# Delta rule in a four-layer decoder trunk: keys first, and one inversion of all sixteen systems on VectorE

## The chip, the core and the metric

The kernel runs on one core of one Trainium2 chip. A core has a matrix engine (TensorE; in the profile PE, with its weight loads as PEld), a vector engine (VectorE, DVE), an activation engine (ScalarE, ACT), a general engine (GpSimd, POOL) and a queue engine (SyncE, SP) that issues the transfers of this kernel. The metric is the device time of one execution in microseconds; lower is better. Before the change three runs took 1253.02, 1254.41 and 1255.75 us.

## The reference, cut to what matters

Four layers, each `x += mixer(rmsnorm(x))`, then `x += conv_ffn(rmsnorm(x))`, for 256 tokens of width 1024. Layer 2 has the mixer that changes, a gated delta rule with 8 heads of width 128:

```python
proj = h @ w_in                                   # queries, keys, values, gates
qkv = silu(causal_dwconv(proj[..., :3 * d], conv_w))
a_mat = where(strict, (k_beta @ k.T) * decay, 0)  # per head and chunk
t_mat = triangular_solve(a_mat + eye, eye)        # its inverse
u = t_mat @ v_beta
w = t_mat @ (k_beta * exp(gc))
v_new = u_i - w_i @ state                         # chunk by chunk
o_i = q_i @ state + a_i @ v_new
state = state * sd_i + k_i.T @ v_new
out = (rmsnorm(o) * silu(z)) @ w_o
```

The kernel takes chunks of 128 tokens, so there are 8 heads times 2 chunks = 16 unit triangular systems of 128 unknowns, each of which has to be inverted before the values can be corrected.

## The kernel before, in words

**Products.** All weights stream from DRAM in chunks of 8 tiles of 128x128 (`Stream`, L102). SP loads a chunk into `wraw` (L128, 4 buffers); ScalarE rounds it into `whi` (L150) and VectorE takes the exact rest `wlo` (L151), at most 5 chunks ahead of their use (L161). A tile costs TensorE three matmuls of 256 columns (L360 to L362); all of TensorE's instructions are recorded on the helper lines L252 and L255.

**Order.** TensorE's instruction order is written out by hand by `Weave` (L169): products are the fill, and every other step is a generator that yields what it cost TensorE and what it waits for, a time by the plan's own clock or a name. When the plan's clock reaches that point, the step's next instructions are put into TensorE's order, whether or not the data will be there by then. The other engines' orders, and SP's, come from a scheduler that goes by the order of the program and by what is ready.

**The delta rule** (`gdn`, L551). Sixteen jobs of 16 tiles each (L17: q0 to q7, then v and z mixed) make, with `queries_keys` (L650), queries and keys of one head per job, with `values` (L825) and `gate` (L943) two heads per job. On VectorE a job takes one multiply out of PSUM (L653, L832) and six steps of two convolutions (L392). `gates` (L578) and `decays` (L632) make write strengths and decay matrices. The heads are worked on in two halves of four (`half`, L892):

- `lengths` (L662): four transposes a head, then squares with sums on ScalarE (L680).
- `systems` (L696): one product a chunk gives the system and the scores together (L705, scaled on VectorE at L709). The systems go to DRAM (L717).
- `invert` (L726): the blocks of 16 on the diagonals come back one block to a partition, 64 partitions (L732). GpSimd inverts them by substitution (L740 to L745). The result goes to DRAM (L747) and returns as rows (L750).
- `join16` (L762): inverses of blocks of 32 from those of 16: two products for every system (L769, L780), with masks on VectorE (L723, L772, L789) and transposes (L760).
- `join_half` (L798): blocks of 64, then of 128.
- then the corrections of both chunks (L903 to L935), the norm (`finish`, L868) and the output's parts (`output`, L950).

The last product (`residual`, L368) takes its first half of rows once heads 0 to 3 are done ("o0") and its second half once heads 4 to 7 are ("o1").

Of the kernel before, what the change touches and what calls it, by code (L numbers as in the profile page):

```python
# [9 lines left out]
F32 = mybir.dt.float32  # L10
# [18 lines left out]
BLK = 16  # L29
NB = 6  # L30
# the jobs of the delta rule's products, in their order
GDN_FILL = "q0 q1 q2 q3 q4 q5 q6 q7 v0 z0 v1 v2 v3 z1 z2 z3"
PRIO = (1, 0)
# [6 lines left out]
L_QK, L_V, L_LEN, L_SYS, L_BLOCKS, L_JOIN, L_XI, L_PM, L_OUT = 6.0, 6.0, 1.0, 0.5, 6.0, 13.0, 1.0, 2.5, 1.0  # L40

# columns of the packed per-channel parameters
# [9 lines left out]
# columns of the shape-only constants  # L52
# [5 lines left out]
C_BD = C_NEG + P  # L58
C_LV = C_BD + P
C_UP = C_LV + P  # L60
C_EO = C_UP + P
C_ST = C_EO + 2
# [3 lines left out]
def constants():  # L66
# [11 lines left out]
    b = i // BLK  # L78
    c[:, C_BD:C_BD + P] = b[:, None] // 2 == b[None, :] // 2
    lower = (b[:, None] == b[None, :] + 1) & (b[:, None] % 2 == 1)  # L80
    c[:, C_LV:C_LV + P] = np.where(lower, -1.0, 0.0)
    c[:, C_UP:C_UP + P] = lower.T
    c[:, C_EO:C_EO + 2] = b[:, None] % 2 == np.arange(2)[None, :]
# [14 lines left out]
# the heads whose queries and keys are made at the same time: the first products follow x as it comes  # L98
# [3 lines left out]
class Stream:  # L102
    """The weights, 8 tiles of 128x128 to a chunk, in the order of their use.

    A chunk is loaded ahead of its use and split into two parts that one pass of the tensor
    engine carries each: hi is w rounded to 12 bits, lo the exact rest."""
# [49 lines left out]
    def take(self, n=1):  # L156
        """The next n tiles side by side: (hi, lo), each [128, n * 128]."""
# [59 lines left out]
def trunk(ctx: ExitStack, tc: tile.TileContext, xT, wstream, pvec, cst, wba, hv, out):  # L217
# [15 lines left out]
    half8 = keep.tile([P, 2, 8], F32, name="half8")  # L233
# [3 lines left out]
    warm = keep.tile([P, 8], F32, name="warm")  # L237
# [9 lines left out]
    class Tensor:  # L247
        """The tensor engine; remembers its last instruction."""
# [9 lines left out]
    # the tensor engine's clock rises while the first data comes  # L258
# [6 lines left out]
    def after(inst):  # L265
        """No earlier in the order of its engine than the tensor engine's last instruction."""
# [30 lines left out]
    def squares(n, apart=KB):  # L297
        """The squares of block n, added to the others' unless n is one of the last, kept apart."""
# [43 lines left out]
    def product(ps, n, rh, rl):  # L342
        """ps[128, 256] += the next n tiles, against rh[k] + rl[k]."""
# [24 lines left out]
    def residual(n_k, rh, rl, gain, order, needs=None):  # L368
        """x += the product, in the order of the plan."""
# [18 lines left out]
    def conv(y, u, taps):  # L388
        """y = causal depthwise convolution of u along its free axis; taps: columns, last first."""
# [156 lines left out]
    # With b the write strength, D the decays between the tokens of a chunk and k the keys before  # L546
    # they are scaled to unit length, the chunk's corrections w solve a unit lower triangular system
    # (I + s_j k_i.k_j D_ij) w = r; s_j = b_j / |k_j|^2 makes up for the lengths. All four heads' systems
    # of a half are worked on together; the blocks of 16 on their diagonals are inverted by
    # substitution, one block to a partition, and joined into larger ones by products.  # L550
    def gdn(gain):  # L551
        nm = Norm()
        NS = 2 * G_H
        with tc.tile_pool(name="gdn", bufs=1) as pool, \
# [17 lines left out]
            def big(dt=F32):  # L572
                return pool.tile([P, NS, P], dt, name="big", bufs=NB)
# [4 lines left out]
            def gates():  # L578
# [44 lines left out]
                for s in halves:  # L623
                    yield from decays(s)
# [463 lines left out]
```

## Time and profile before

| | |
|---|---|
| Median of 3 runs | 1254.41 us |
| The profiled execution, first to last instruction (its span; no other time of it is given) | 1253.2 us |
| TensorE matmuls, busy | 1236.0 us |
| VectorE, busy | 945.0 us |
| ScalarE, busy | 730.2 us |
| GpSimd, busy | 103.4 us |
| TensorE's clock, mean | 0.991 |
| The delta rule on TensorE: first product to last | 581.7 to 760.4 us |

Matmuls are pipelined: in the timeline a matmul of 256 columns lasts 0.28 us, but the next one begins 0.12 us later. Costs on TensorE are therefore taken from the distance of starts and not from durations. The same holds, to a smaller degree, for VectorE. "Idle before" is time in which an engine had nothing to do just before an instruction; the name behind the arrow is what it waited for last.

### The profile page before, as it was taken

What the parts mean: (1) busy time and instruction counts of PE and PEld (TensorE: products, weight loads), DVE (VectorE), ACT (ScalarE), POOL (GpSimd) and SP (SyncE); (2) the same over time, 40 slices, a digit from 0 to 9 for tenths busy, and PEclk for the clock granted to TensorE, in tenths of its full rate; (3) what the DMA queues carried; (4) which work ended last, traced back from release to release, by engine and by line L of the source; (5) the groups of instructions that cost most, each with busy time, mean ns of one, the idle gap of its engine ahead of it and who ended that gap; (6) DMA issues with size and microseconds to landing.
All of it is one profiled execution on the core that took longest, in us unless ns stands there. A gap on an engine that the chain in (4) does not pass through costs nothing.

```text
span 1253.2 us, 25399 instructions
## 1 busy us (share of the span) xinstructions
PE 1236.0 (99%) x10222; PEld 1218.7 (97%) x10222; DVE 945.0 (75%) x1532; ACT 730.2 (58%) x1259; POOL 103.4 (8%) x147
## 2 busy tenths in 40 slices
PE   9999999999999999999998999999999999999997
PEld 8989999999999999999997999999999989999997
DVE  7756999856877999855995568999665756999842
ACT  6655766544445666545873666666554655766641
POOL 2002000001002000002055002000011002000000
PEclk9999999999999999999997999999999999999998
DMA  8655565656656556665444345666655445565650
GB/s 293 195 155 165 185 185 185 185 185 185 185 185 182 177 188 183 195 183 176 130 126 127 87 135 157 201 184 186 187 187 181 153 160 167 178 185 186 184 185 35
DMA packets 67430, 216.01 MB, mean 172 GB/s; under 512 B 11248, under 2 KB 14832, under 8 KB 67312
## 3 DMA queue, kind: packets, MB, share of 16 engines
q1 hardware_dynamic: 67024, 213.86, 55.1%
q8 instruction: 80, 1.31, 0.4%
q10 hardware_dynamic: 288, 0.52, 0.1%
q14 instruction: 38, 0.31, 0.1%
HBM read 212.13 MB, written 2.23 MB: 171 GB/s over the span
## 4 chain that ended last, share of the span: by engine, by line
PE 90%; DVE 4%; ACT 2%; issue 2%; POOL 1%; DMA 1%; SPq 0%; POOLq 0%; DVEq 0%; ACTq 0%
PE mm L252 84%; PE sm L252 5%; DVE wlo L151 1%; PE sm L255 1%; DVE xl L290 1%; DVE yqk L392 1%; POOL xm L743 1%; ACT whi L150 1%; POOL xb L745 1%; ACT jk L680 0%; DMA wraw<-wstream 0%; DVE x L380 0%; DVE big L643 0%; DMA xc<-d 0%; ACT yqk L658 0%
## 5 line engine op out<-in xcount | busy, mean ns | idle before, releaser
L151 DVE TENSOR_TENSOR wlo<-wraw,whi 128x1024 fp32r<-128x1024 f32 (+1 forms) x404 | 490.5, 1214 | 198.3 <-ACT whi L150 197.1
L252 PE MATMUL mm<-xh,whi 128*128 128x256 f32 x2112 | 603.4, 286 | 0.0
L252 PE MATMUL mm<-xl,whi 128*128 128x256 f32 x2112 | 595.9, 282 | 0.7 <-DVE xl L290 0.7
L252 PE MATMUL mm<-xh,wlo 128*128 128x256 f32 x2112 | 595.7, 282 | 0.6 <-DVE wlo L151 0.6
L150 ACT CAST whi<-wraw 128x1024 fp32r<-128x1024 f32 (+1 forms) x404 | 420.2, 1040 | 294.3 <-PE mm L252 264.2
L252 PEld LDWEIGHTS mm<-xl,whi 128*128 128x128 f32 x2112 | 400.1, 189 | 1.8 <-DVE xl L290 1.1
L252 PEld LDWEIGHTS mm<-xh,wlo 128*128 128x128 f32 x2112 | 399.8, 189 | 1.3 <-DVE wlo L151 1.0
L252 PEld LDWEIGHTS mm<-xh,whi 128*128 128x128 f32 x2112 | 400.0, 189 | 1.1 <-ACT whi L150 0.3
L252 PE MATMUL mm<-ah,whi 128*128 128x256 f32 x704 | 198.1, 281 | 0.0
L252 PE MATMUL mm<-ah,wlo 128*128 128x256 f32 x704 | 198.1, 281 | 0.0
L252 PE MATMUL mm<-al,whi 128*128 128x256 f32 x704 | 198.1, 281 | 0.0
L392 DVE SCALAR_TENSOR_TENSOR y<-u,pv,y 128x255 f32<-128x255 f32 (+1 forms) x352 | 146.0, 478 | 0.0
L252 PEld LDWEIGHTS mm<-ah,whi 128*128 128x128 f32 x704 | 132.5, 188 | 0.0
L252 PEld LDWEIGHTS mm<-al,whi 128*128 128x128 f32 x704 | 132.5, 188 | 0.0
L252 PEld LDWEIGHTS mm<-ah,wlo 128*128 128x128 f32 x704 | 132.5, 188 | 0.0
L304 POOL TENSOR_TENSOR sq<-sq 128x256 f32<-128x256 f32 x62 | 51.2, 825 | 980.0 <-ACT sq L302 978.1
L385 ACT CAST ah<-a 128x256 fp32r<-128x256 f32 x88 | 35.7, 406 | 99.8 <-DVE a L412 99.8
L390 ACT ACTIVATE y<-u,pv 128x256 f32<-128x256 f32 x176 | 79.6, 500 | 8.6 <-DVE u L405 8.6
L405 DVE TENSOR_TENSOR u<-mm,rb 128x512 f32<-128x512 f32 x88 | 60.5, 688 | 2.7 <-PE mm L252 1.3
L290 DVE SCALAR_TENSOR_TENSOR xl<-x,pv,xh 128x256 fp32r<-128x256 f32 x64 | 53.2, 862 | 3.1 <-ACT xh L289 3.1
L410 ACT ACTIVATE y<-y 128x256 f32<-128x256 f32 x88 | 36.6, 418 | 19.6 <-DVE y L392 17.4
L380 DVE TENSOR_TENSOR x<-x,mm 128x512 f32<-128x512 f32 (+1 forms) x36 | 22.4, 623 | 24.6 <-PE mm L252 24.6
(197 smaller groups left out, 1145.0 us busy)
## 6 DMA issues: line engine op xcount, KB each, us to landing
wraw<-wstream SPq DMA_DIRECT2D x396, 512.0 KB, 3.6
wraw<-wstream SPq DMA_DIRECT2D x8, 256.0 KB, 4.5
x<-xT SPq DMA_DIRECT2D x8, 128.0 KB, 4.3
d<-aq SPq DMA_DIRECT2D x2, 512.0 KB, 3.6
out<-xg ACTq DMA_DIRECT2D x2, 256.0 KB, 2.3
cs<-cst SPq DMA_DIRECT2D x1, 329.0 KB, 6.4
pv<-pvec SPq DMA_DIRECT2D x1, 324.5 KB, 5.5
cs<-cst SPq DMA_DIRECT2D x1, 320.0 KB, 5.6
```

The source lines that it names most:

```text
L150: self.nc.scalar.copy(hi[:, s], raw[:, s])
L151: self.nc.vector.tensor_sub(lo[:, s], raw[:, s], hi[:, s].bitcast(F32))
L252: self.last = nc.tensor.matmul(*a, **k)
L255: self.last = nc.tensor.transpose(*a, **k)
L290: V.scalar_tensor_tensor(xl[n], xn, col(gain + n), xh[n].bitcast(F32), op0=ALU.mult, op1=ALU.subtract)
L304: G.tensor_add(sums[0], sums[0], sq)
L380: V.tensor_add(xn, xn, pss.pop(n)[:, :w * T].rearrange("p (g t) -> p g t", g=w))
L385: S.copy(dst_h, src)
L390: S.activation(y, u, AF.Copy, scale=col(taps[0]))
L392: V.scalar_tensor_tensor(y[:, d:], u[:, :T - d], col(c), y[:, d:], op0=ALU.mult, op1=ALU.add)
L405: V.tensor_mul(u, pairs(ps), nm.rb2)
L410: S.activation(y[:, 0, :], y[:, 0, :], AF.Silu)
```

## The change

The jobs become k0 to k3, v0 to v3, q0 to q3, z0 to z3, with two heads in each. The keys of all heads come first, and only keys are needed for the systems. `keys` multiplies keys by keys and takes the squared lengths from that product's diagonal, on VectorE; it scales the system on VectorE and stores the four diagonal blocks of 32 with one transfer each. `queries` makes the scores apart from the systems. `invert` works on all 16 systems at once, 64 blocks of 32, each on two partitions that hold its even and its odd rows, so that all 128 partitions are used; the substitution is 31 steps of two instructions, now on VectorE. `join16` with its masks, `am`, `pm` and its products is gone. `join_half` takes 16 systems instead of 8. The result of the joins leaves PSUM through VectorE for `xt` and through ScalarE for `xi`. Some instructions are marked to go ahead of their place in the program (`tc.high_priority()`).

```diff
-BLK = 16
-GDN_FILL = "q0 q1 q2 q3 q4 q5 q6 q7 v0 z0 v1 v2 v3 z1 z2 z3"
+BLK = 32
+GDN_FILL = "k0 k1 k2 k3 v0 v1 v2 v3 q0 q1 q2 q3 z0 z1 z2 z3"
+L_GATES, L_KEYS, L_QK, L_V, L_BLOCKS, L_JOIN, L_XI, L_OUT = 8.0, 3.0, 6.0, 6.0, 6.0, 8.0, 2.0, 1.0
...
+            def keys(n, ps):
+                yield 0, ("norm",)
+                y = kk[:, n:n + 2, :]
+                mixed(1, n, ps, y)
+                yield 0, ("decays",)
                 S.activation(y, y, AF.Silu)
+                yield 0, L_KEYS
...
+                for i in range(4):
+                    h, ts = n + i // 2, slice(i % 2 * P, (i % 2 + 1) * P)
+                    PE.matmul(pk[:, i * P:(i + 1) * P], lhsT=kk[:, h, ts], rhs=kk[:, h, ts], start=True, stop=True)
...
+                with tc.high_priority():
...
+                        V.tensor_tensor_reduce(out=jk, in0=pk[:, i * P:(i + 1) * P], in1=ident, scale=1.0, scalar=0.0,
+                                               op0=ALU.mult, op1=ALU.add, accum_out=ln[:, 1, m:m + 1])
+                    V.tensor_scalar(le[:, 1, ms], ln[:, 1, ms], EPS, None, op0=ALU.add)
+                    V.reciprocal(sk[:, ms], le[:, 1, ms])
...
+                        V.scalar_tensor_tensor(aq[:, m, :], pk[:, i * P:(i + 1) * P], sk[:, m:m + 1],
+                                               dt[:, m, :], op0=ALU.mult, op1=ALU.mult)
+                    for b in range(NQ):
+                        bs = slice(b * BLK, (b + 1) * BLK)
...
+                            nc.sync.dma_start(out=o["d1"][b, ms].rearrange("m j c -> j m c"), in_=aq[bs, ms, bs])
+                wv.set(f"k{n}", LAG)
+                yield 0.9, L_KEYS
...
+            def invert():
...
+                yield 0, tuple(f"k{n}" for n in range(0, H, 2))
+                G.tensor_tensor(rn[:, 1, :], le[:, 1, :], half8[:, 1, :], op=ALU.pow)
+                wv.set("lengths", 2 * LAG)
+                for s in range(2):
+                    nc.sync.dma_start(out=bl[s * 64:(s + 1) * 64], in_=o["d1"].rearrange("b m j c -> (b m) j c"))
+                yield 0, L_BLOCKS
+                busy = 0.0
+                for k in range(BLK - 1):
+                    n, r = k // 2 + 1, BLK - 1 - k
+                    m = xm[:, :n * r].rearrange("p (n r) -> p n r", n=n)
+                    first = V.tensor_mul(m, xb[:, :n, k:k + 1].to_broadcast([P, n, r]),
+                                         bl[:, k:k + 1, k + 1:].to_broadcast([P, n, r]))
+                    if busy == 0:
+                        after(first)
+                    V.tensor_sub(xb[:, :n, k + 1:], xb[:, :n, k + 1:], m)
+                    busy += 2 * (0.16 + n * r / 960)
+                    if busy > 2.5 or k == BLK - 2:
+                        yield 0, 1.5 * busy
+                        busy = 0.0
+                d2 = dram.tile([2, NQ, NS, BLK // 2, BLK], F32, name="d2")
+                nc.sync.dma_start(out=d2.rearrange("s b m i c -> (s b m) i c"), in_=xb)
...
+                    for b in range(NQ):
+                        for s in range(2):
+                            nc.sync.dma_start(out=x32[b * BLK + s:(b + 1) * BLK:2],
+                                              in_=d2[s, b].rearrange("m i c -> i m c"))
+                yield 0, L_JOIN
...
+                    after(V.transpose(xi32.rearrange("p m i -> p (m i)"), x32.rearrange("p m i -> p (m i)")))
...
+                yield 0, L_XI
+                yield from join_half(BLK, (0, 64), (0,), lambda r, m: xi32[r, m, :], lambda r, m: x32[r, m, :], xi, xt)
+                yield from join_half(64, (0,), (), lambda r, m: xi[:, m, :], lambda r, m: xt[r, m, r], xi, xt)
+                wv.set("inverse", LAG)
```

## Rows read from the trace of the kernel before

**Rows 1.** The page, busy time (share of the span) and instructions of each engine.

```profile
PE 1236.0 (99%) x10222; PEld 1218.7 (97%) x10222; DVE 945.0 (75%) x1532; ACT 730.2 (58%) x1259; POOL 103.4 (8%) x147
```

**Rows 2.** The chain of waits, 636 to 668 us: start, length, what.

```profile
637.85 2.92 DMA d<-aq
640.79 2.75 DMA bl<-d
...
660.34 1.96 DMA d<-xb
662.31 3.19 DMA xc<-d
```

**Rows 3.** Timeline of PE: start, length, form, count, [idle before, releaser].

```profile
581.73 0.28 PE L252 MATMUL mm<-xh,whi 128*128 128x256 f32 x1
...
627.60 0.65 PE L255 MATMUL sm<-cs,yqk 128*128 128x128 f32 x4 [1.03 <-ACT yqk L658]
...
633.97 0.65 PE L255 MATMUL sm<-cs,yqk 128*128 128x128 f32 x4 [0.28 <-ACT jk L680]
...
666.58 3.56 PE L252 MATMUL sm<-xi,big 128*128 128x16 f32 x16 [4.32 <-DVE xi L760]
...
679.06 1.07 PE L252 MATMUL sm<-xi,aq 32*32 32x32 f32 x32 [0.46 <-DVE xi L760]
...
684.31 0.69 PE L252 MATMUL sm<-xt,m 32*32 32x32 f32 x16 [0.84 <-ACT big L817]
...
760.33 0.28 PE L252 MATMUL mm<-big,wlo 128*128 128x256 f32 x1
```

**Rows 4.** Stretches: busy time of each engine, TensorE's clock, DMA share, GB/s.

```profile
592.80:637.80 45.00, 43.68 (x356) 42.56 (x355) 41.03 (x95) 39.65 (x99) 3.43 (x2) 1.00 0.43 132
...
655.00:660.00 5.00, 5.00 (x37) 4.79 (x37) 4.93 (x12) 2.72 (x6) 4.29 (x10) 1.00 0.00 0
...
665.00:670.00 5.00, 3.42 (x17) 3.45 (x17) 2.86 (x5) 0.98 (x1) 1.11 (x1) 0.50 0.99 369
670.00:675.00 5.00, 5.00 (x24) 5.00 (x25) 3.05 (x3) 1.01 (x2) 0.49 (x3) 0.50 0.57 112
```

**Rows 5.** Timeline of PE, a product of `join16` and what follows it.

```profile
698.61 1.85 PE L252 MATMUL sm<-xi,big 128*128 128x16 f32 x16
700.31 1.14 PE L252 MATMUL sm<-m,kt 128*128 128x128 f32 x8
```

**Rows 6.** The chain of waits, a stretch of layer 1 with products alone.

```profile
404.23 184.05 PE mm L252 x1554
```

**Rows 7.** Timeline of DVE, the four kinds of its larger work.

```profile
592.84 0.69 DVE L653 TENSOR_TENSOR u<-mm,rb 128x512 f32<-128x512 f32 x1 [2.79 <-ACT rb L337]
...
611.93 3.44 DVE L643 SCALAR_TENSOR_TENSOR big<-sm,gc,cs 128x128 f32<-128x128 f32 x13
...
618.16 2.45 DVE L392 SCALAR_TENSOR_TENSOR yqk<-u,pv,yqk 128x255 f32<-128x255 f32 x6
...
641.84 2.36 DVE L151 TENSOR_TENSOR wlo<-wraw,whi 128x1024 fp32r<-128x1024 f32 x2
```

**Rows 8.** Groups by line and form, DVE: busy us, mean ns of one.

```profile
L455 DVE CUSTOM_DVE_ANT_0 p<-sm,nb 128x128 f32<-128x128 f32 x16 | 4.6, 290 | 9.8 <-PE sm L252 8.0 <-PE sm L255 1.7
...
L455 DVE DVE_READ_ACCUMULATOR2_ANT st<- 128x1 f32 x32 | 2.7, 83 | 0.0
...
L782 DVE TENSOR_TENSOR xt<-xt,sm 128x128 f32<-128x128 f32 x2 | 0.6, 288 | 2.5 <-PE sm L252 2.5
...
L691 DVE TENSOR_TENSOR sk<-sk,bt 128x8 f32<-128x8 f32 x2 | 0.3, 168 | 0.1
```

**Rows 9.** Timeline of SP, the store and the load after the inversion.

```profile
660.34 0.49 SPq L747 DMA_DIRECT2D d<-xb  x1
...
662.31 0.38 SPq L750 DMA_DIRECT2D xc<-d  x1
```

**Rows 10.** Timeline of ACT, the weight rounding at 665 us.

```profile
664.94 1.04 ACT L150 CAST whi<-wraw 128x1024 fp32r<-128x1024 f32 x1 [5.49 <-DMA wraw<-wstream]
```

More of the change, by code (lines that the diff above doesn't have):

```diff
@@ L648, in decays @@
-                wv.set(f"d{s.h0}")
-            def queries_keys(h, ps):
-                yield 0, ("norm",)
+                    with tc.high_priority():
+                        for i in range(4):
+                            h, t = divmod(m0 + i, 2)
+                            V.scalar_tensor_tensor(dt[:, m0 + i, :], pd[:, i * P:(i + 1) * P],
+                                                   gc[:, t, h:h + 1], cs[:, C_NEG:C_NEG + P],
+                                                   op0=ALU.subtract, op1=ALU.add)
@@ new lines, in gates, with mixed @@
+                    yield 0.9, 0
+                with tc.high_priority():
+                    V.tensor_sub(dl, gc[:, 2, :], gc[:, 0, :])
+                    for m in (0, H):
+                        S.activation(dt[:, m:m + H], dt[:, m:m + H], AF.Exp)
+                    S.activation(dl, dl, AF.Exp)
+                    S.activation(eg, gc[:, 1, :], AF.Exp)
+                    V.tensor_scalar(neg, eg, -1.0, None, op0=ALU.mult)
+                wv.set("decays")
+            def mixed(q, n, ps, y):
@@ L833, in values @@
+            def values(n, ps):
+                yield 0, ("norm",)
                 y = pool.tile([P, 2, T], F32, name="u", bufs=4)
-                for q in range(2):
-                    conv(y[:, q, :], u[:, q, :], taps(2, h + q))
+                mixed(2, n, ps, y)
                 S.activation(y, y, AF.Silu)
                 yield 0, L_V
-                yield 0, (f"l{s.h0}",)
+                yield 0, ("lengths",)
+                if n == 0:
+                    o["r"] = big().rearrange("p (t a) i -> p t a i", t=2)
@@ new lines, in m4, with heads @@
+            def m4():
+                return pool.tile([P, G_H, P], F32, name="m4", bufs=NM)
+            def heads(s, one):
+                ps = bank("sm")
+                for a in range(G_H):
+                    one(ps[:, a * P:(a + 1) * P], G_H * s + a)
+                return ps
+            def solve(s, t):
+                pw = heads(s, lambda p, h: PE.matmul(p, lhsT=o["xt"][:, 2 * h + t, :], rhs=o["r"][:, t, h, :],
+                                                     start=True, stop=True))
+                w = m4()
@@ L887, in finish @@
[L887 to L901 removed]
+                V.tensor_mul(f[:, 1, :], f[:, 1, :], rq)
@@ L903, in half @@
                 w = solve(s, 0)
                 yield 0.87, LAG
-                pst = bank("sm")
-                for a in range(G_H):
-                    PE.matmul(pst[:, a * P:(a + 1) * P], lhsT=s.kt[:, a, :], rhs=w[:, a, :], start=True, stop=True)
-                st = pool.tile([P, G_H, P], F32, name="m4", bufs=6)
-                S.copy(st.rearrange("p a i -> p (a i)"), pst)
-                po = scores(s, 0, w)
-                yield 1.74, LAG / 2
-                wv.add(finish(s, 0, po.rearrange("p (a i) -> p a i", a=G_H)))
@@ L923, in half @@
[L923 to L928 removed]
+                pst = heads(s, lambda p, h: PE.matmul(p, lhsT=kt[:, h, :], rhs=w[:, h % G_H, :], start=True, stop=True))
@@ new lines, in chunks @@
+                st = m4()
+                S.copy(st.rearrange("p a i -> p (a i)"), pst)
+                yield 0.87, (f"q{G_H * s}", f"q{G_H * s + 2}")
+                wv.add(finish(s, 0, four(scores(s, 0, w))))
+                yield 0.87, LAG / 2
+                ps = heads(s, lambda p, h: PE.matmul(p, lhsT=kk[:, h, P:], rhs=st[:, h % G_H, :], start=True, stop=True))
+                for a in range(G_H):
+                    h = G_H * s + a
+                    V.scalar_tensor_tensor(o["r"][:, 1, h, :], ps[:, a * P:(a + 1) * P], neg[:, h:h + 1],
+                                           o["r"][:, 1, h, :], op0=ALU.mult, op1=ALU.add)
@@ L929, in half @@
+                pq = heads(s, lambda p, h: PE.matmul(p, lhsT=qq[:, h, P:], rhs=st[:, h % G_H, :], start=True, stop=True))
+                qs = m4()
+                V.tensor_mul(qs, four(pq), eg[:, hs].unsqueeze(2).to_broadcast([P, G_H, P]))
                 yield 1.74, LAG
@@ L971, in fill @@
                     yield from products([ps], range(KB), KB, xh, xl)
-                    if job == "q0":
+                    n = 2 * int(job[1:])
+                    if job == "k0":
                         wv.add(nm.steps())
                         wv.add(gates())
-                        for n in PRIO:
-                            wv.add(half(halves[n]))
-                    n = int(job[1:])
-                    wv.add({"q": queries_keys, "v": values, "z": gate}[job[0]](n if job[0] == "q" else 2 * n, ps))
+                        wv.add(invert())
+                        for s in range(2):
+                            wv.add(chunks(s))
+                    wv.add({"k": keys, "q": queries, "v": values, "z": gate}[job[0]](n, ps))
                 yield from residual(KB, yhs, yls, gain, PLAN_HALVES, {0: ("o0",), KB // 2: ("o1",)})
```

482 lines of the change are left out of this document (184 added, 298 removed).

## The prediction, on record before the changed kernel was run

> **What bounds the kernel now.** I read the page first. TensorE's matmuls are busy 99% of the span, its weight loads 97%, VectorE 75% [rows 1]. Read alone, this says that work taken from TensorE is won and work given to VectorE is free. But the share is a mean over all layers, so the next view is the delta rule's own stretches. It runs on TensorE from 581.7 to 760.4 us, 178.7 us in all [rows 3]. In the 45 us from its first norm on, VectorE is busy 41.03 and ScalarE 39.65 [rows 4]: two engines nearly full beside TensorE. Third, the chain of waits. From the last system at 637.85 it runs through two transfers of 2.92 and 2.75 us, GpSimd's substitution until 660.34, and two more transfers of 1.96 and 3.19 [rows 2]. It is that chain for which TensorE waits 4.32 us at 666.58; with four smaller waits it stands still 1.03 + 0.28 + 4.32 + 0.46 + 0.84 = 6.9 us [rows 3]. Behind the long wait its granted clock is 0.50, the 1.2 GHz level, from 665 to 675, in which it works 3.42 + 5.00 = 8.4 us [rows 4]; at the 2.4 GHz level that work takes half, so 4.2 us are lost.
>
> **What TensorE gains.** `join16` goes. One of its four products over 8 systems takes 700.31 - 698.61 = 1.70 us at full clock [rows 5], so 6.8 us. Key and query products cost the same in two pieces of 128 columns as in one of 256 (I take it so from the columns). 24 transposes of keys and queries stand where 32 stood: four take at most 0.65 [rows 3], so 8 give up to 1.3, and I take 0.7, as they overlap. If no wait at all were left, the delta rule would take 178.7 - 6.9 - 4.2 - 6.8 - 0.7 = 160.1 us. The most to be won is thus 18.6 us.
>
> **Where TensorE stands in its new order.** Its order is fixed by the plan's clock. Adding up the plan's yields by hand gives the places: all four key products behind tile 70 of the 256 tiles of fill, the values' transposes behind tiles 102, 116, 132 and 148, the scores of the first two query jobs behind 164 and 178, and the first product of the joins behind tile 188. A tile is three matmuls of 184.05 / 1554 = 0.118 us [rows 6], 0.355 us. Up to the joins TensorE has 188 tiles, 66.8 us; 40 products for decays, keys and scores, four in at most 1.14 us [rows 5] and in 0.95 as they overlap, 9.5; 32 transposes at 0.1, 3.0; norm, gates and changes of kind, by estimate 5.2 (what before needs beyond tiles and products). The sum is 84.5, so without a wait it is there at 666.2 us, and has 160.1 - 84.5 = 75.6 us behind it.
>
> **What VectorE must have done by then.** Since TensorE's order holds the values' transposes and two score products ahead of the joins, VectorE has to finish all of this first, in whatever order. It begins at 592.84 with the first multiply [rows 7].
> - Weight parts: 24 chunks used, 8 of them made before: 16 at 1.14 us (two in 2.36, the overlap counted once) [rows 7]: 18.2.
> - Convolutions of ten jobs (4 keys, 4 values, 2 queries): 0.69 and 2.45 [rows 7], which overlap their neighbours; I take 3.0 a job: 30.0. These are the same before and after, only earlier or later.
> - Decays, 16 at 3.44 / 13 = 0.265 [rows 7], and nine small steps of the gates at 0.17 [rows 8]: 5.7.
> - New for keys: 16 squared lengths at 0.29 + 0.08 [rows 8], from ScalarE; 16 scalings of systems at 0.265; 16 small steps at about 0.2: 13.3.
> - Scores of the first query job, 4 at 0.265: 1.1.
> - The inversion, from GpSimd: 31 steps of two instructions. An instruction of 8 elements takes 0.168 us, of 128 elements 0.288 [rows 8], so 0.16 and 1.0 ns an element. The steps' sizes, (k // 2 + 1)(31 - k), add up to 2856, twice that is 5712: 62 x 0.16 + 5.7 = 15.6. Bounds: 11.9, if each overlaps its neighbour by 0.06, and 17.9, if each takes the 0.288 of 128 elements.
> - The 32x32 transposes over 512 elements, like the 0.69 of another 512: 0.7.
>
> The sum is 84.6. Its idle time was 45 - 41.03 = 4.0 in the first 45 us [rows 4], and I leave it. So the joins can't start before 592.8 + 84.6 + 4.0 = 681.4 us, 15 us after TensorE could be there. What was on GpSimd and ScalarE, and cost nothing, now stands in the queue that feeds TensorE. The masks that go with `join16` would have fallen partly behind this point.
>
> **What else the path gets.** The four stores of a key job and eight loads in place of one stand in SP's queue, 0.38 us an issue [rows 9]. After the inversion: store 1.96, eight issues 3.0, landing 2.8 (3.19 less its issue) [rows 2, 9], 7.8 us before the joins' first operand. If VectorE still has needed work then, this costs nothing; if all of it stood earlier in its order, 7.8. The plan has one query job at that place, so I take half, 3.9. The stores of the first key jobs and the return of the blocks (2.92 and 2.75, [rows 2]) I cost at nothing: the values' convolutions cover them; without these it would be 5.7. Before the joins TensorE now waits 681.4 + 3.9 - 666.2 = 19.1 us in all. Its clock fell behind 4.32, so I take one such fall, 4.2, between none and two (8.4). Behind it I keep the two small waits of the old joins, 0.46 + 0.84 [rows 3]: 1.3. GpSimd keeps only small powers and clears; nobody waits for its old loop.
>
> **Sum.** The last product ends at 681.4 + 3.9 + 75.6 + 4.2 + 1.3 = 766.4 in place of 760.4: 6.0 us later. The profiled span is 1253.2, so 1259.2; the median of the runs stands 1.2 above that span, so 1260.4. With all bounds at one end it is 1260.4 - 3.7 - 3.9 - 4.2 = 1248.6, at the other 1260.4 + 2.3 + 3.9 + 4.2 = 1270.8.
>
> **Rivals.** A measurement of this kernel can tell about 0.2%, 2.5 us.
> - *Faster: VectorE is not the bound.* If its small steps overlap more than I think, or less has to precede the joins, TensorE keeps only waits like those of before: 160.1 + 6.9 = 167.0, which is 11.7 us less: 1242.7. The place is the first product of the joins, and it decides if that starts before about 673 (666.2 + 6.9). For it speaks that VectorE is only 75% busy overall and that 6.8 us of TensorE's work are certainly gone [rows 1, 5]; against it the 41.03 of 45 [rows 4]. The Trainium skill ("Perfetto Trace Analysis", Identifying the Most-Contended Engine) judges by the highest occupancy, for TensorE by its weight loads; by its 97% against VectorE's 75% this rival would be the one to come, and only its remark on regimes in the next section (Optimization Strategy) leads to my reading. Chance 0.26.
> - *No change.* VectorE is late as reckoned, but the transfers are covered and the waits fall in pieces behind which the clock stays up: 681.4 + 75.6 + 1.3 = 758.3, 2.1 less: about 1252 to 1254. Chance 0.17.
> - *Slower still: weights starve.* SP takes its queue in order. Before, the store after the inversion stood in it until 660.34; from 655 to 660 the DMA share is 0.00, and ScalarE then waited 5.49 us for weights [rows 4, 9, 10]. An inversion stretched by other work to some 38 us (from about 641), against 9 loaded or split chunks of 2.84 us (25.6), leaves 12 us without weights; as it lies beside waits already counted, I take 11 on top: 1271. Chance 0.12.
> - That the change does not do what it says has no chance worth a number: `join16` and GpSimd's loop are plainly gone.
>
> **Numbers.** The forecast, 1260.4, has 0.45; its own range is 1249 to 1271. Slower has 0.45 + 0.12 = 0.57, no change 0.17, faster 0.26. The range for 8 in 10 goes from 1243, which leaves out half of the faster rival, to 1272, which leaves out about half of the last.
>
> **What would show it.** Right: VectorE busy over 90% from 593 to 680; the values' convolutions or weight parts between the inversion's steps; the inversion spread over 30 us or more; a wait of TensorE for VectorE ahead of the key products or the joins, over 10 us together, with clock 0.50 behind it; the first join near 685. Wrong: the first join before 673, or an inversion in one piece of 16 us with TensorE busy beside it. I would also be wrong if the scheduler let convolutions go ahead so early that the waits fall where nothing is lost.

## The result, and the profile after

The changed kernel takes 1272.83 us (median of 4 runs), the kernel before 1254.72 beside it: ratio 1.0145, 95% interval 1.0132 to 1.0157, some 18 us slower. The forecast was 1260.4, its range ended at 1272. The profiled execution has a span of 1270.5 us and took 1272.59.

The page of the changed kernel, first part:

```profile
PE 1228.3 (97%) x10182; PEld 1211.6 (95%) x10182; DVE 951.9 (75%) x1642; ACT 716.9 (56%) x1214; POOL 77.3 (6%) x86
```

Beside [rows 1] TensorE has 7.7 us less work, VectorE 6.9 more, ScalarE 13.3 less. VectorE's share is 75% in both. The shares do not show the loss; the delta rule's own rows do.

Timeline of PE, the delta rule's first and last product and its larger waits (in brackets: idle time before, and who ended it):

```profile
580.26 0.28 PE L242 MATMUL mm<-xh,whi 128*128 128x256 f32 x1
...
616.89 1.16 PE L242 MATMUL sm<-kk 128*128 128x128 f32 x8 [2.50 <-ACT kk L660]
...
626.09 2.08 PE L242 MATMUL sm<-kk 128*128 128x128 f32 x8 [8.04 <-ACT kk L660]
...
696.09 1.91 PE L242 MATMUL sm<-xi,big 32*32 32x32 f32 x32 [17.18 <-DVE xi L798]
698.68 1.91 PE L242 MATMUL sm<-xi,big 32*32 32x32 f32 x32 [0.68 <-ACT m L826]
...
707.20 1.91 PE L242 MATMUL sm<-x,m 32*32 32x32 f32 x32 [0.83 <-DVE big L836]
...
734.24 1.16 PE L242 MATMUL sm<-m,kk 128*128 128x128 f32 x8 [1.40 <-DVE big L907]
...
779.32 0.28 PE L242 MATMUL mm<-big,wlo 128*128 128x256 f32 x1
```

The delta rule takes 779.32 + 0.12 - 580.26 = 199.2 us, against 178.7 [rows 3]: 20.5 more. The waits above and four under 0.5 us add up to 31.9, against 6.9: 25.0 more. What TensorE works is 199.2 - 31.9 = 167.3 against 171.8: 4.5 less, `join16` gone and more half clock added. So TensorE did win what was taken from it, and lost over five times as much by standing still. Outside the delta rule the two spans differ by 3.2 us the other way, and among all profiles here by up to 5.0; so the runs below are compared by the delta rule's length first.

Stretches of the changed kernel: busy us (and instructions) of PE, PEld, DVE, ACT, POOL, then TensorE's clock, DMA share, GB/s:

```profile
593.00:642.00 49.00, 38.46 (x303) 38.05 (x304) 40.95 (x136) 27.16 (x45) 2.90 (x1) 0.86 0.37 106
642.00:684.40 42.40, 36.34 (x306) 35.73 (x304) 42.35 (x123) 25.87 (x59) 0.17 (x1) 0.99 0.47 146
684.40:697.00 12.60, 0.91 (x17) 0.92 (x18) 2.39 (x5) 1.02 (x2) 0.77 (x1) 0.50 0.33 83
697.00:713.00 16.00, 14.49 (x183) 13.94 (x181) 6.86 (x14) 5.58 (x15) 0.00 (x0) 0.61 0.11 34
713.00:779.40 66.40, 64.30 (x572) 63.28 (x571) 40.70 (x65) 38.93 (x86) 9.22 (x8) 0.99 0.37 112
```

From 642 to 684.4 VectorE is busy 42.35 of 42.40 us. Then all engines stand nearly still for 12.6 us, and behind that TensorE's clock is 0.61. After 697 VectorE is busy little more than half. What fills it before, timeline of DVE:

```profile
642.19 0.18 DVE L776 TENSOR_TENSOR xm<-xb,block 128x31 f32<-128x31 f32 x1
642.29 0.48 DVE L382 SCALAR_TENSOR_TENSOR u<-u,pv 128x255 f32<-128x255 f32 x1
642.68 0.18 DVE L780 TENSOR_TENSOR xb<-xb,xm 128x31 f32<-128x31 f32 x1
642.79 0.48 DVE L382 SCALAR_TENSOR_TENSOR u<-u,pv 128x255 f32<-128x255 f32 x1
...
684.20 0.19 DVE L780 TENSOR_TENSOR xb<-xb,xm 128x16 f32<-128x16 f32 x1
691.31 0.42 DVE L801 COPY big<-x 32x512 f32<-32x512 f32 x1 [6.93 <-DMA x<-d]
...
695.32 0.71 DVE L798 STREAM_TRANSPOSE xi<-x 128x512 f32<-128x512 f32 x1 [0.97 <-DMA x<-d]
```

Behind nearly every step of the inversion (L776, L780) stands one instruction of another job, 0.34 to 1.22 us (the longest is a weight part, the exact rest `wlo` of a chunk). Groups of DVE from 592.6 to 684.3, columns as in [rows 8]:

```profile
L776 DVE TENSOR_TENSOR xm<-xb,block 128x126 f32<-128x126 f32 (+22 forms) x31 | 7.7, 249 | 0.0
L780 DVE TENSOR_TENSOR xb<-xb,xm 128x126 f32<-128x126 f32 (+22 forms) x31 | 7.7, 249 | 0.0
...
L672 DVE CUSTOM_DVE_ANT_0 jk<-sm,cs 128x128 f32<-128x128 f32 x16 | 4.5, 283 | 3.3 <-PE sm L242 3.2
...
L672 DVE DVE_READ_ACCUMULATOR2_ANT ln<- 128x1 f32 x16 | 1.3, 81 | 0.0
```

The inversion's 62 instructions last 15.4 us and are spread over 42. VectorE overlaps neighbours (642.19 to 642.29 for 0.18), so from start to start they cost it only 10.2 us, the squared lengths (L672) 3.7 instead of 5.8; both sums are over all rows of DVE up to 684.4, and all of them together give 83.6.

VectorE also stood idle for 8 us in this stretch, more than half of it behind TensorE's late key products (timeline of DVE):

```profile
628.20 0.29 DVE L672 CUSTOM_DVE_ANT_0 jk<-sm,cs 128x128 f32<-128x128 f32 x1 [2.89 <-PE sm L242]
634.45 0.69 DVE L651 TENSOR_TENSOR u<-mm,rb 128x512 f32<-128x512 f32 x1 [1.97 <-PE mm L242]
```

The queue of SP behind the inversion:

```profile
684.46 0.33 SPq L786 DMA_DIRECT2D d<-xb  x1
688.32 5.24 SPq L793 DMA_DIRECT2D x<-d  x8
```

From the last step's end, 684.39, to the first join, 696.09, are 11.7 us: 3.9 until the store has landed, 5.24 for eight issues (0.66 each, where [rows 9] has 0.38), 1.8 until the last load is there, 0.8 for the transpose.

### The profile page after: what moved, and what is told of

It reads as the page before. It is cut to its first block, busy times and chain, and to the rows that moved or that the text cites. A ratio compares the mean times of both kernels' runs of the same rounds, so it can differ in the third digit from the quotient of the medians.

```text
span 1270.5 us, 25350 instructions
## 1 busy us (share of the span) xinstructions
PE 1228.3 (97%) x10182; PEld 1211.6 (95%) x10182; DVE 951.9 (75%) x1642; ACT 716.9 (56%) x1214; POOL 77.3 (6%) x86
## 4 chain that ended last, share of the span: by engine, by line
PE 88%; DVE 7%; issue 2%; ACT 1%; DMA 1%; SPq 1%; POOL 0%; POOLq 0%; DVEq 0%; ACTq 0%
PE mm L242 82%; PE sm L242 5%; DVE wlo L141 2%; DVE xl L280 1%; PE sm L245 1%; DVE u L382 0%; DVE x L370 0%; ACT whi L140 0%; DVE xm L776 0%; DMA x<-xT 0%; DVE qq L382 0%; SPq L793 0%; POOL f L879 0%; DVE xb L780 0%; DMA d<-xb 0%
```

## The experiments

**The theory** at the start: VectorE's queue ahead of the joins is the bound, and what stands in it is paid for one to one; the transport behind lies open. **Rivals:** the inversion's own chain is late and VectorE has room; the transport or the weights decide; the clock does.

| kernel | delta rule, us | TensorE's waits | first join | median | ratio to before, 95% |
|---|---|---|---|---|---|
| changed | 199.2 | 31.9 | 696.1 | 1272.83 | 1.0132 to 1.0157 |
| inversion in one piece | 199.7 | 34.0 | 696.4 | 1274.38 | 1.0143 to 1.0177 |
| gates ahead of queries | 212.6 | 39.2 | 691.2 | 1286.83 | 1.025 to 1.0281 |
| loads from two queues | 195.4 | 28.7 | 693.5 | 1271.23 | 1.0123 to 1.0159 |
| key posts, plain priority | 195.5 | 28.3 | 692.5 | 1270.18 | 1.0115 to 1.0145 |
| one piece, TensorE asks later | 195.3 | 26.9 | 687.3 | 1269.28 | 1.0104 to 1.0136 |
| joins later | 193.8 | 23.3 | 703.0 | 1268.86 | 1.0093 to 1.0137 |
| dummy products | 195.9 | 15.5 | 695.1 | 1271.24 | 1.0117 to 1.0155 |
| 29 steps left out | 181.9 | 15.4 | 679.8 | 1256.51 | 1.0005 to 1.0024 |
| weight parts on GpSimd | 201.6 | 30.4 | 698.7 | 1274.09 | 1.013 to 1.0174 |
| lengths on ScalarE | 193.6 | 28.1 | 695.8 | 1270.47 | 1.0113 to 1.0144 |
| several together | 187.5 | 17.0 | 686.0 | 1261.20 | 1.0041 to 1.0078 |
| inversion on GpSimd | 195.0 | 27.4 | 692.2 | 1269.96 | 1.011 to 1.015 |
| several, later still | 192.0 | 21.0 | 688.0 | 1265.59 | 1.0079 to 1.0137 |

(First join: the time in that profile; the delta rule's start differs by up to 2.5 us among them. Waits: those of 0.15 us and more within the delta rule.)

The lengths, waits and joins are each those of one execution. By the times, only the gates' order, the steps left out and the several edits together are clear of the changed kernel's interval; for the other edits the traces show what moved, and the gain in time is not shown beyond noise.

### The inversion in one piece

```diff
-                    if busy == 0:
-                        after(first)
+                    with tc.high_priority(): ...
+                yield 0, 1.5 * busy
...
+                if "inv" in o:   # a later job's multiply goes behind the last step
+                    tc.add_manual_dep(first.ins, o["inv"].ins.name, ...)
```

> The 31 steps of the inversion stand in one piece in VectorE's order, and the values' and queries' jobs that come later in the program go behind it; the work is the same. Theory (VectorE's queue is the bound, and the transport behind the inversion lies open because nothing is left beside it): the inversion ends near 660 to 664 instead of 684.2, the transport of some 12 us runs beside the convolutions, but the values and the first two query jobs then still take VectorE 22 us, so TensorE waits about as long as before, only at the values' transposes, and the first product of the joins comes at 684 to 686 instead of 696.1: about 11 us less, 1261 to 1263. Rival (the chain of steps alone is late, VectorE has room): joins without a wait from 679, 17 us and the half clock less, 1250 to 1255. Rival (order doesn't matter, the sum of the work does): 1272.

The last step starts at 660.7, as expected (views of the second instruction of a step, and of TensorE); the time did not come down.

```profile
L784 DVE TENSOR_TENSOR xb<-xb,xm x31: 186/264/299, 641.2 to 660.7; 128x126 f32<-128x126 f32 x3, 128x30 f32<-128x30 f32 x2, 128x56 f32<-128x56 f32 x2, 128x78 f32<-128x78 f32 x2
```
```profile
665.28 1.12 PE L245 MATMUL sm<-cs,u 128*128 128x128 f32 x4 [18.95 <-ACT u L733]
```

The wait went from the joins to the values' transposes, and grew. The rival that the chain alone is late falls: with the inversion 23.5 us earlier nothing was won. But my 11 us fell too. The steps, next to nothing but each other, now cost VectorE 17.6 us (19.9 less two weight parts of 1.14) instead of 10.2; TensorE stood so long at the transposes that it reached the joins no earlier; and the last loads stood behind weight loads in SP's queue (one issue each at 671.49, 675.10 and 678.60), which is the queue my starving rival spoke of; here they cost nothing, as TensorE did not wait at the joins.

### Less other work in the queue, a shorter transport, another order of the key jobs

```diff
-GDN_FILL = "k0 k1 k2 k3 v0 v1 v2 v3 q0 q1 q2 q3 z0 z1 z2 z3"
+GDN_FILL = "k0 k1 k2 k3 v0 v1 v2 v3 z0 z1 z2 z3 q0 q1 q2 q3"
```

(`rn` is computed in two halves there, as the first is needed before the last queries.)

> The four gate jobs go ahead of the four query jobs, so that before the joins VectorE has four multiplies (2.4 us) in place of three query jobs (18 convolution steps at 0.40, three multiplies, eight scores at 0.27: 11.2 us). Theory (VectorE's queue): the inversion's last step comes 8 to 9 us earlier, near 675.5, and the joins as well, near 687; the time falls by 6 to 9 us, 1264 to 1267, less if the late queries hold up the scores behind the joins. Rival (the inversion's own chain of dependent steps sets its end): it still ends at 682 or later and the time stays at 1272 or gets worse.

The last step came at 679.4, 4.8 us earlier where 8 to 9 were expected, and the late queries held up the chunks: waits of 7.21 and 1.8 to 2.1 us behind 749, 13 us lost. A miss on the time, a half on the mechanism.

```diff
-                            nc.sync.dma_start(out=x32[...],
+                            (nc.sync, nc.scalar)[s].dma_start(out=x32[...],
```

> Of the eight loads behind the inversion four are issued by ScalarE's queue, four by SP's. Theory (each issue lies open on the path to the joins): 4 x 0.65 us less in series, the joins 2 to 2.6 us earlier, 1270 to 1271. Rival (the data's landing or a wait elsewhere decides): no change, 1272.8.

The wait at the joins is 14.84 instead of 17.18, the first join 2.6 us earlier, as expected: from the last step's end to it are 9.35 us instead of 11.70. The medians' gain is within their spread.

```diff
                 ms = slice(2 * n, 2 * n + 4)
-                with tc.high_priority():
+                if True:
```

> The work behind the key products (squared lengths, systems, their stores) loses its high priority, so that the fourth key job's convolution goes ahead of most of it. Theory (VectorE's order held the last key product up, and VectorE then stood idle for 2.9 and 2.0 us itself): TensorE's wait ahead of the last key product falls from 8.0 us to under 3, the joins come some 5 us earlier, 1266 to 1269. Rival (VectorE is behind anyway, the wait only moves to the joins): TensorE's waits add up to the same and the time stays within 1 us of 1272.8.

The last key product waits 2.46 instead of 8.04 us; the joins come 3.6 us earlier and wait 18.31, more than before. The high priority of the posts (the work behind a key product: lengths, systems, stores) had held up the last key convolution, as the theory said, but the median misses its range by 1.2, and only half of the 3.6 us is the keys'. The last step ended 1.8 us earlier, at 682.6. The other 1.8 came behind it: the store landed in 2.0 us instead of 3.9. Timeline of SP:

```profile
682.70 0.33 SPq L786 DMA_DIRECT2D d<-xb  x1
684.71 5.23 SPq L793 DMA_DIRECT2D x<-d  x8
```

The changed kernel had issued a weight load 0.5 us before this store, this one had issued none for 2.8 us. All fourteen kernels with this inversion agree: 3.2 to 4.3 us in the eight with a weight load issued within 1 us before the store, 2.0 to 2.4 in the six others.

### TensorE's order, the clock, the inversion's whole price

```diff
-L_QK, L_V = 6.0, 6.0
+L_QK, L_V = 20.0, 28.0    # with the inversion in one piece
```

> The inversion in one piece as in the run before, and now the values' transposes and the queries' scores also stand later in TensorE's order (allowances 28 and 20 us instead of 6 and 6; the values' tiles take the gates' buffers so that four can be alive). Theory now (VectorE has enough time in the whole stretch; what costs is that TensorE's fixed order asks for results before VectorE can have them, with fill left over that could stand there): the wait of 18.95 us at the values' transposes goes, waits of some 5 us stay behind tile 184, and with the wait goes the half clock behind it: 1250 to 1259. Rival (the sum of VectorE's work ahead of the joins is the bound, wherever TensorE waits): 1268 to 1275, with a wait of 15 us or more at the joins or the scores.

```profile
666.61 0.55 PE L242 MATMUL mm<-xh,whi 128*128 128x256 f32 x1 [9.96 <-DVE u L651]
```

The waits at the transposes are gone, and the fill itself now waits, 9.96 us, for a place in PSUM: VectorE did not take the finished products out while it inverted. The wait has a third place, with the same engine at its end. The time, 1269.28, is the rival's; the place is neither's.

```diff
-L_JOIN = 8.0
+L_JOIN = 26.0
```

> The changed kernel with one number changed: the plan's allowance ahead of the joins is 26 us instead of 8, which puts their first product behind tile 236 of the fill instead of 190. Theory now: the wait of 17.2 us at the joins falls to 2 us or less and the clock behind it stays up, but the chunks' steps then have 20 tiles of fill (7 us) between them instead of 54 (19 us), so up to 12 us of their waits come to light: 1261 to 1268. Rival (VectorE's sum of work): the joins wait 15 us or more all the same, 1272 or more.

The joins wait 0.68 us, as expected, and 5.4 us are won. Waits of 3.09 (scores, for queries), 4.16 and 2.24 (the last norm and the output) came to light. So a third of the 17 us was won; the median misses its range by 0.9.

```diff
+                for _ in range(38):
+                    PE.matmul(bank("sm")[:, :T], lhsT=idle[:, :P], rhs=idle, start=True, stop=True)
                 yield from join_half(BLK, ...
```

> The changed kernel with 38 products on zeros in TensorE's order just ahead of the joins, in the time in which TensorE waits; their results are not used. This prices the clock: work at 0.50, 0.67 and 0.80 of the clock from 690 to 720 us lost 1.6 + 3.0 + 2.0 = 6.6 us. Theory (TensorE's clock lengthens the path behind the wait): clock 1.00 behind the joins' start, 1266 to 1268. Rival (behind the joins the other engines set the pace, the clock costs nothing): 1272 to 1273.

Stretches, columns as above:

```profile
684.40:697.00 12.60, 11.40 (x81) 9.76 (x80) 2.38 (x5) 1.29 (x3) 0.05 (x1) 1.00 0.29 78
697.00:713.00 16.00, 14.99 (x208) 14.34 (x209) 6.86 (x14) 6.81 (x18) 0.00 (x0) 0.79 0.11 35
```

The clock was 1.00 up to the joins and fell behind them all the same, to 0.79 over 16 us (0.61 without the dummies). 15.0 x 0.79 - 14.5 x 0.61 = 3.0 us; the delta rule is 3.3 shorter. So the half clock due to the wait is worth 3 us, not 6.6. The median, 1271.24, lies between the theory's range and the rival's, and shows this only as a trend.

```diff
+                    if k in (0, BLK - 2):
                         first = V.tensor_mul(m, ...
```

> 29 of the 31 steps of the inversion are left out (the first and the last stay, so that stores and loads keep their places); the inverse is not that of the systems. Theory (VectorE's queue): 14.6 us of VectorE's work are gone, the last step comes near 668 instead of 684.2, the joins near 680, TensorE's wait there goes from 17.2 to about 1 us and the half clock with it: 1249 to 1255. Rival (transport or weights hold the joins up): over 1262.

```profile
679.77 0.40 PE L242 MATMUL sm<-xi,big 32*32 32x32 f32 x7 [2.63 <-DVE xi L798]
```

The delta rule is 17.3 us shorter and the joins come 16.3 us earlier; the median, 1256.51, misses its range by 1.5. This is the run that settles the main cause, the inversion on VectorE. It does not tell the inversion's work from its place in the queue; the first run shows that another place alone wins nothing. Nor is it "one to one", as I had it: VectorE is busy 130.4 us in the delta rule instead of 139.3, 8.9 us less (58 instructions, overlapped), but the last step comes 20.6 us earlier (timeline of DVE):

```profile
663.60 0.18 DVE L780 TENSOR_TENSOR xb<-xb,xm 128x16 f32<-128x16 f32 x1
```

Work of other jobs that had stood between the steps now stands behind the last one. From its end to the first join are 16.0 us, more than the 11.7 before, but they lie beside convolutions, and TensorE waits 2.63 us at their end. Without waits this kernel's delta rule is 181.9 - 15.4 = 166.5 us; even without the inversion it is no faster than before, because the key jobs alone wait 2.50 and 7.47 us.

### Where else the work could go

```diff
+                low = self.nc.gpsimd if self.shared and c % 2 else self.nc.vector
-                self.nc.vector.tensor_sub(lo[:, s], ...
+                low.tensor_sub(lo[:, s], ...
```

> In the delta rule's jobs before the joins every second chunk's rest (eight in all) is taken by GpSimd instead of VectorE; nothing else changes. Theory (what stands in VectorE's queue ahead of the joins is paid for one to one, whatever it is): 8 x 1.14 = 9.1 us less on VectorE, the inversion's last step near 675.5, the joins near 688, the delta rule 7 to 9 us shorter than the 199.2 of the changed kernel, 1264 to 1267. GpSimd takes 0.82 us for 256 elements, so some 3.3 us for a chunk of 1024, which is needed only every 5.7 us. Rival (GpSimd is too slow or gets in VectorE's way): TensorE waits for GpSimd's rests, or VectorE's instructions grow, and the time is 1271 or more.

GpSimd was fast enough (2.39 us for most chunks), and in VectorE's way. Timelines of POOL and DVE:

```profile
650.02 2.69 POOL L143 TENSOR_TENSOR wlo<-wraw,whi 128x1024 fp32r<-128x1024 f32 x1 [4.25 <-ACT whi L141]
```
```profile
650.37 2.42 DVE L782 TENSOR_TENSOR xb<-xb,xm 128x56 f32<-128x56 f32 x1
```

An instruction of VectorE that takes 0.21 us took 2.42, ending with GpSimd's. The rival held.

```diff
-                        V.tensor_tensor_reduce(out=jk, in0=pk[...], in1=ident, ..., accum_out=ln[...])
+                        S.activation(jk, pt[:, i * P:(i + 1) * P], AF.Square, accum_out=ln[...])
```

> The keys' squared lengths go back to ScalarE: four transposes a key job ahead (two of them are the kernel's own, moved), squares with sums there as before the change; VectorE loses 16 products with the diagonal (4.5 + 1.3 us). Theory (VectorE's queue, one to one): the joins 5 to 6 us earlier, the delta rule 4 to 6 us shorter, 1267 to 1269. Rival (the extra transposes and ScalarE's squares lengthen the chain of the key jobs, the two cancel): 1271 to 1274.

The delta rule is 5.6 us shorter, the size expected, but not in the way expected, so the size is luck; the median, 1270.47, misses its range by 1.5. TensorE waits less at the keys (5.8 instead of 10.5 us) and more at the joins (19.21). Counted from the delta rule's start, the inversion's last step ended at 103.95 us, against 104.13 in the changed kernel: it did not move. The place of the squared lengths was filled by work that the joins do not need, a fourth query job and a 22nd weight part, and VectorE was busy 84.0 us up to the last step instead of 83.7. Groups of DVE up to it, in the changed kernel and in this one:

```profile
L382 DVE SCALAR_TENSOR_TENSOR qq<-u,pv,qq 128x255 f32<-128x255 f32 (+2 forms) x18 | 8.6, 480 | 0.0
L382 DVE SCALAR_TENSOR_TENSOR qq<-u,pv,qq 128x255 f32<-128x255 f32 (+2 forms) x24 | 11.8, 491 | 0.0
```

The joins came 2.1 us earlier, as the store landed in 2.1 us instead of 3.9. The other 3.5 us came behind the joins, with the clock at half for 10.8 us there instead of 14.5 and 0.8 us less of waits.

```diff
-                    first = V.tensor_mul(m, ...
+                    first = G.tensor_mul(m, ...
-                    V.tensor_sub(xb[...], ...
+                    G.tensor_sub(xb[...], ...
```

> The changed kernel with only the 31 steps of the inversion put on GpSimd, nothing else. In the kernel before, GpSimd's steps took 0.23 us for 28 and 0.37 us for 64 elements and about 0.08 us between two, so 62 steps with 5712 elements take about 36 us undisturbed, 41 with some held up. Theory (VectorE's queue, one to one, with the inversion's own chain as the next limit): VectorE has 15.4 us less, but the inversion ends near 678 to 684 as it does now, so the delta rule stays at 195 to 200 us and the time at 1268 to 1273. Rival (only VectorE's load counts): 182 to 185 us, 1254 to 1258, as with the steps left out.

```profile
L780 POOL TENSOR_TENSOR xb<-xb,xm x31: 221/464/1314, 641.6 to 679.9; 128x126 f32<-128x126 f32 x3, 128x30 f32<-128x30 f32 x2, 128x56 f32<-128x56 f32 x2, 128x78 f32<-128x78 f32 x2
```

As expected: 39.6 us from 640.3, the delta rule at 195.0. A block of 32 in this form is too long a chain for GpSimd, where a block of 16 was hidden [rows 2].

### Everything that helped, together

The inversion in one piece with convolutions alone held behind it, `L_KEYS, L_QK, L_V = 5.0, 20.0, 28.0`, lengths on ScalarE, loads from two queues:

> Several edits together: the inversion in one piece with only multiplies and weight parts beside it (the convolutions of later jobs go behind it), the values' transposes and the queries' scores later in TensorE's order, key products 2 us later, squared lengths on ScalarE, the loads behind the inversion from two queues. Theory (two causes: VectorE's queue ahead of the joins, and TensorE's order that asks too early; both are eased here): the inversion ends near 665, the joins start near 677 to 682, TensorE's waits add up to 10 to 15 us instead of 31.4, the delta rule takes 180 to 188 us instead of 199.2: 1253 to 1261. Rival (VectorE's sum of work is the bound in any order): 193 us or more, 1267 or more.

```profile
674.09 1.11 PE L245 MATMUL sm<-cs,z 128*128 128x128 f32 x4 [7.47 <-ACT z L732]
...
685.96 1.91 PE L242 MATMUL sm<-xi,big 32*32 32x32 f32 x32 [3.02 <-DVE xi L799]
```

11.7 us won, more than any one edit but leaving the steps out, and still slower than the kernel before. The delta rule is within its range, near the slow end; the inversion ended at 671.0 and not near 665, and the joins (686.0), the waits (17.0) and, by 0.2, the median lie outside theirs. Then `L_QK, L_V, L_JOIN = 24.0, 36.0, 14.0`, and multiplies and weight parts first:

> As the kernel with several edits together (delta rule 187.5 us, three waits of 3.6, 7.5 and 3.0 us), with TensorE's order later still: values' transposes from tile 194 instead of 168, joins behind tile 218 instead of 200; multiplies and weight parts of the value and query jobs get high priority on VectorE. Theory (what is left is TensorE's order asking too early): the waits of 7.5 and 3.0 us go, some 6 us of waits appear among the chunks' steps, which have 38 tiles of fill instead of 56 between them, the clock falls less: delta rule 179 to 184 us, 1252 to 1257. Rival (VectorE's sum of work up to the joins is now the bound): TensorE waits as long as before, for weight parts, multiplies or the joins, and the delta rule stays at 186 to 190 us, 1260 or more.

```profile
675.00 0.66 PE L247 MATMUL sm<-cs,z 128*128 128x128 f32 x4 [1.44 <-ACT z L735]
685.17 2.07 PE L244 MATMUL sm<-qq,kk 128*128 128x128 f32 x8 [5.95 <-ACT qq L706]
...
745.99 1.31 PE L244 MATMUL mm<-big,whi 128*128 128x256 f32 x2 [5.21 <-ACT big L377]
```

The rival held, and at 192.0 us the delta rule is longer than even it had it: asked later, VectorE delivered no earlier (the queries at 685), and the chain behind the joins came out at the end, 5.21 us before the last product. VectorE is busy 55.5 of the 60 us from 630 to 690 in this run, 56.0 in the one before. What was not tried: the 16-blocks of before in the new order of the keys, which would keep GpSimd's loop short.

## Why the prediction was right in direction and too small in size

By the steps of the prediction, all in the profiled execution:

- **TensorE's floor, 160.1 us: right within some 3 us.** The rows give 167.3 us without waits in the changed kernel and 166.5 with the steps left out. The excess over 160.1 is half clock: TensorE worked 19.7 us at the lower level, and half of it, 9.9 us, is what that cost. At full clock it would have worked 157.4. Of the 2.7 us between, 1.7 are a second fall in the kernel before, 3.4 us of work at 0.50 from 685.5 on, which the prediction had not taken off. The stretches at 0.50 in the changed kernel, columns as above:

```profile
618.40:632.10 13.70, 6.01 (x28) 6.01 (x29) 10.50 (x56) 2.69 (x6) 2.32 (x1) 0.50 0.20 52
683.30:703.70 20.40, 6.94 (x79) 6.74 (x80) 4.51 (x14) 3.26 (x6) 0.94 (x1) 0.50 0.21 52
707.10:714.00 6.90, 6.80 (x58) 6.51 (x59) 3.28 (x8) 0.67 (x3) 0.00 (x0) 0.51 0.24 76
```

- **TensorE at the joins by 666.2: wrong.** It came at 678.9 (696.09 - 17.18), as the key products had waited 10.5 us. I had looked for VectorE's total and not at the order in it: the posts of the first key jobs went ahead of the last key convolution. VectorE set the joins' start, so the late TensorE cost nothing there directly; it did through VectorE, which stood idle 2.89 and 1.97 us for the late key products. With the posts at plain priority VectorE's idle time up to the last step was 5.5 us instead of 8, and that step came 2.0 us earlier, counted from the delta rule's start.
- **VectorE's work, 84.6 us and 4.0 idle, joins not before 681.4: the sum near, its parts not.** The last step ended at 684.39, 3.0 late, behind 83.6 us of work and 8 of idle time instead of 4.0. But the inversion cost 10.2 and not 15.6 (outside its bounds, 11.9 to 17.9, as neighbours overlap by more than 0.06), the squared lengths 3.7 and not 5.9. In their place stood work that the joins did not need: 21 weight parts instead of 16 (23.9 us; the parts ahead of their use, which I had left out), a third query job and four more scores. The sum of needed work was not the bound; the queue that put other work between all steps was. The run with the lengths on ScalarE shows it: needed work went, other work took its place, and the last step stayed.
- **The transport, "I take half, 3.9", between 0 and 7.8: the step that failed.** It took 11.7 us, and all of it counted. Two errors: the prediction let VectorE's queue and the transport overlap by a half, though a queue that puts another job's work behind every step has nothing left to cover what follows the last one; and the price was short, 0.38 us an issue for loads that take 0.66, and 1.96 for a store that takes 3.9 behind a weight load of 512 KB. (With no load just ahead the same store took 2.0: issued at 660.96, loads from 662.97, in the run with one piece.) Issues and store are 4.1 us over their price, the landing 1.0 under. The 11.7 also has 0.8 for the transpose, which the prediction counted with VectorE's work. The step is 7.8 of the 10.8 us by which the joins were later than forecast (696.1 against 685.3).
- **Behind the joins 75.6 + 4.2 + 1.3 = 81.1: 83.35.** The sum is near because two errors cancel. The small waits were 3.6, not 1.3. The clock cost 6.9 (13.7 us worked at 0.50), not 4.2, and the work itself would have taken 72.9 at full clock, not 75.6.

3.0 + 7.8 + 2.3 = 13.0: the delta rule ended at 779.4 instead of 766.4. The part behind the delta rule took 1.7 us less than before, so the span is 11.3 over the forecast of 1259.2, and the median of the runs stood 2.3 above the span instead of 1.2: 12.4 in all. The range had the transport at 7.8 at most, and so ended just short.

**The rivals.** *Faster*: the joins started far behind 673; the engine with the highest occupancy of the whole run was not the bound. The Trainium skill ("Perfetto Trace Analysis", Optimization Strategy) says that the most-contended engine may change over time; here the rows agree, 42.35 of 42.40 us for VectorE in one stretch at 75% overall. *Weights starve*: TensorE waited for no weight product in the delta rule; SP's queue cost in another way, as the loads' issues. *No change* had the transfers covered and the waits in pieces; neither came.

**The signs.** Inversion over 30 us, convolutions between its steps, TensorE over 10 us late for VectorE at the keys and joins, half clock behind: all there. VectorE was over 90% busy from 593 to 680 (78.95 of 87.0), and the join near 685 was not.

What is shown: the inversion's share (left out, 17.3 of the 20.5 us come back), and that the 11.7 us of transport lay open behind it, of which a second queue takes 2.3 and a store with no weight load just ahead 1.8. The key jobs' share is near 2 us at the last step; the delta rule is 3.7 us shorter with plain priority, but half of that is the store. The parts do not add up, as each moves the next wait. What is only argued: that the whole loss is a matter of these three and the clock, and that the order of VectorE's queue weighs more than its sum in the time itself; no run eased all to the point at which TensorE did not wait.

## What to carry to other kernels

Count what an engine's queue will hold *before* the point where another engine waits, in that stretch alone and with work that is only made ahead of its use; then add in full whatever follows in series behind the last step of a chain: where other work stands between all its steps, it ends last, and nothing is left to cover its transport. Taking 6.8 us from the engine that is busy 99% is worth nothing if a chain of 62 steps goes to one at 75% that is full just there. Taking work out of a queue does not move the end of a chain in it if work of later jobs takes the place. An order that asks later helps only as far as the late engine has work that can wait; here that was 5.4 of 20 us by itself, and 11.7 together with other edits.

## What was not expected of the hardware

- **VectorE stands still while GpSimd reads.** A weight part of 1024 elements on GpSimd, 2.4 to 2.7 us, held VectorE's two-input steps up to its end (1.93 and 2.42 us for one instead of 0.2 to 0.3). One took 3.50 us, beside a weight part of VectorE that took its usual 1.22. With the inversion on GpSimd, VectorE's weight parts took 1.33 us instead of 1.22 and its convolutions 0.57 to 0.59 instead of 0.48 on average (640 to 690 us). The Trainium skill ("SBUF — State Buffer", Who interferes with whom) says that a VectorE instruction with two inputs in SBUF contends with a GpSimd one that reads SBUF, that such contention is an exclusive lock, and that the order of issue decides who blocks. The rows agree. That this is the whole reason why half the weight parts were no gain on GpSimd is argued: TensorE also waited 3.99 us at a key product instead of 2.50, and the first step of the inversion came 5 us later.
- **The clock fell without a wait ahead.** With dummy products up to 694 TensorE had no wait over 1.01 us behind 679, and its clock was 0.79 from 697 to 713, in the joins' products of 32x32. With the joins placed later (0.68 us of wait) it was 0.78 from 704.2 to 720. So the lower level went with the small products themselves; no run tells them apart from the gaps of 0.5 to 1.0 us that stand among them.
- **An issue is not a fixed price.** SP needed 0.66 us for a load of 32 values a row into every second partition, 0.38 for the single load of before [rows 9]. Nor is a store's landing: 2.0 to 2.4 us, or 3.2 to 4.3 right behind a weight load.
- **A small step's price depends on its neighbour.** Among other jobs' instructions the inversion's 62 cost VectorE 10.2 us, 0.16 each from start to start; next to each other, every one in need of the one before, 17.6 us, 0.28 each. So one piece ends earlier, and costs VectorE 7 us more.
